# Broadcasts and scores over 128 rows, and a 31-tap convolution as column-group products, in a two-block network on one core

## The chip, the core and the metric

The kernel runs on 1 core of a Trainium2 chip. The metric is device time in microseconds (us), the median of the runs. TensorE is called PE in the profile, and PEld where it loads weights; VectorE is DVE, ScalarE is ACT, GpSimd is POOL, SyncE is SP.

## What is computed

The input `x` is 256 tokens of 1024 float32 numbers. The first block is a Mamba-2 layer (called SSD here), a convolutional feed-forward layer, an attention layer with forget gates (fox), and a second feed-forward layer. The second block puts 16 meta tokens ahead of the sequence (272 positions) and runs a mixer, then a layer of 16384 experts chosen by product keys. Cut to what the change touches:

```python
# SSD, per head: decay between positions of a chunk of 128
decay = exp(where(causal, a_cs[..., :, None] - a_cs[..., None, :], -inf))
# fox, per head
sc = q @ k.T * scale + cum[:, :, :, None] - cum[:, :, None, :]
# mixer of the second block: z = rmsnorm(h) @ w_in
h = a * sigmoid(b)                          # 512 channels, 272 positions
h = depthwise_conv(h, conv_w, taps=31, causal) + conv_b
conv_out = silu(layernorm(h))
attn_out = mla(z_q, z_kv, z_rope)           # 8 heads, low-rank queries and keys
h = h + concat(rmsnorm(attn_out), rmsnorm(conv_out)) @ w_out
# experts: 8 heads, two halves of 64 numbers, 128 keys each
s = einsum('chpd,hpnd->chpn', q, keys); top_k(s, 16) ...
```

## The kernel before

All large products split a float32 weight into a rounded part `hi` (ACT, L128) and a remainder `lo` (DVE, L129), both float32r, and the activations likewise; three float32r products stand for one float32 product. `mm_a` (L136 to L141) has the weights as the stationary operand and 256 or 272 tokens moving; `mm_b` (L143 to L147) has 128 tokens stationary and up to 512 weight columns moving. The stages run one after the other: `ssd`, `ffn(0)`, `fox`, `ffn(1)`, `mix2`, `peer`. Within a stage, `weave` places side work (attention steps, convolution pieces, routing) between weight blocks, and a static scheduler then fixes the order of each engine's instructions; each engine works through its own list in that order. SP issues the weight loads, ACT the small loads.

Broadcasts. `row_parts` (L364) keeps a row per head in a tile of 64 or 48 partitions: the rounded part in the low rows, the remainder 32 rows up. `rowbc` (L372, L375) spreads one head's row over 128 partitions by a product with a 0/1 column `pick` of as many rows. In SSD, `decay` does it for two heads at a time, each followed by a 128-row product that adds the mask (L377): 16 such places for 32 heads. In fox, `bias_item` does it for two heads at a time without the mask, 8 times.

Mixer (`mix2`). `low_rank` multiplies all tokens by 416 columns (L146 and its neighbours); the third tile, which holds the meta tokens, needs only the last 160 of them. `ab(f)` makes one quarter (128 channels) of the convolution's input `U[f]`. The 31 taps of quarter f are split at `PE_TAPS = (4, 4, 6, 31)`: the first ones on PE, where ACT scales an identity by the tap's weights (L821) and PE multiplies the shifted `U[f]` by it in float32 (L822); the others on DVE, one `scalar_tensor_tensor` each (L829). Attention is done in 16 steps of (query tile, head): `scores` (L964), a masked maximum on DVE (L968), two exponentials on ACT (L972, L973), a turn on PE (`flip`, L981), a copy on ACT (L983), `values` (L989). It is woven with the last two `ab` quarters and the convolution of quarters 1 and 2; quarter 3's convolution follows it, then `conv_done` (layer norm) and the output projection `out_proj` with the attention's four row blocks first.

Experts (`peer`). `route` computes the key scores for one token tile: `scores(p, hq)` multiplies 64 rows (half p) for four heads (L1106), 128 keys each, four times per token tile.

```python
            run(low_rank() + B[0])
            weave([queries] + B[1] + [key_values], C[0])
            weave(S, B[2] + C[1] + B[3] + C[2])
            run(C[3])
```

Of the kernel before, what the change touches and what calls it, by code (L numbers as in the profile page):

```python
# [10 lines left out]
F32 = mybir.dt.float32  # L11
F32R = mybir.dt.float32r
# [20 lines left out]
PE_TAPS = (4, 4, 6, 31)  # L33
# [13 lines left out]
for _n, _c in (("ssd_cw", 24 * 4), ("ssd_cb", 24), ("ffn_cw", 2 * FF * 3), ("ffn_cb", 2 * FF), ("c2w", 4 * CONV_K),  # L47
               ("c2b", 4), ("fox_qg", 1), ("fox_kg", 1), ("dt_bias", 1), ("a_log", 1), ("b_f", 1)):
    _cols(_n, _c)
# [17 lines left out]
def tile_body(ctx, tc, A, out):  # L67
# [23 lines left out]
    pick = const.tile([64, 32], F32R, name="pick")  # L91
# [147 lines left out]
    def out_proj(src, nk, yT, keep, fin=residual):  # L239

        acc = [ps_mm.tile([P, 512], F32, name="mm") for _ in range(4)]
        held = []

        def mms(j, w, t, cs=(0, 1)):
            hi, lo = w
            for c in cs:
                mm_b(acc[2 * t + c], yT, j, (t * P, (t + 1) * P), hi[:, c, :], lo[:, c, :], j == 0,
                     j == nk - 1)

        def item(j):  # L250
            h = j - (nk - len(keep))
            w = weight(src[j], 2, keep=keep[h]() if h >= 0 else None)
# [111 lines left out]
    def row_parts(pool, rows, name):  # L364

        n = rows.shape[0]
        r = pool.tile([n, T], F32R, name=name)
        nc.scalar.activation(r, rows, AF.Copy)
        nc.vector.tensor_tensor(r[32:], rows[32:], r[32:].bitcast(F32), op=OP.subtract)
        return r  # L370

    def rowbc(ps, rows, r, more=None):  # L372

        n = rows.shape[0]
        nc.tensor.matmul(ps, lhsT=pick[:n, r:r + 1].to_broadcast([n, P]), rhs=rows, start=True, stop=more is None)  # L375
# [18 lines left out]
    def ssd():  # L394
        with ExitStack() as es:
# [36 lines left out]
            nc.vector.tensor_tensor(pick, ident[:64, :32], ident[:64, 32:64], op=OP.add)  # L432
# [349 lines left out]
    def mix2():  # L782
        with ExitStack() as es:
# [16 lines left out]
            U, CP = {}, {}  # L800

            def ab(f):
                pre = []

                def second():
# [4 lines left out]
                    U[f] = sb.tile([P, TM + CONV_K - 1], F32, name=f"cu{f}")  # L810
                    nc.vector.memset(U[f][:, :CONV_K - 1], 0.0)
                    nc.vector.tensor_tensor(U[f][:, CONV_K - 1:], pre[0], sg, op=OP.mult)
# [3 lines left out]
            def taps_pe(f, j0, j1):  # L816
                if j0 == 0:
                    CP[f] = ps_mm.tile([P, 512], F32, name="mm")[:, :T]
                dg = sb.tile([P, j1 - j0, P], F32, name="dg", bufs=2)
                for j in range(j0, j1):  # L820
                    nc.scalar.activation(dg[:, j - j0, :], ident, AF.Copy, scale=col("c2w", f * CONV_K + j))  # L821
# [581 lines left out]
```

## Time and profile before

| | |
|---|---|
| median of 3 runs | 1724.05 us (1723.29 to 1724.34) |
| the profiled execution: its time, its span | 1724.77 us, 1723.0 us |
| PE busy | 1684.2 us, 98% |
| PEld busy | 1493.3 us, 87% |
| DVE busy | 1259.5 us, 73% |
| ACT busy | 966.2 us, 56% |
| POOL busy | 35.2 us, 2% |
| granted TensorE clock, mean | 0.998 of full speed |
| chain that ended last | PE 91%, DVE 4%, ACT 1%, DMA 1% |

The span is the time from the first to the last instruction of the program on the core; the execution's own time adds what lies around it. A row of the timeline gives the start of an instruction and its duration; products overlap in the array, so the distance between two starts, not the duration, is what a product costs. A float32 product is recorded twice, with half of its time each; a float32r product once.

### The profile page before, as it was taken

What the parts mean: (1) busy time and instruction counts of PE and PEld (TensorE: products, weight loads), DVE (VectorE), ACT (ScalarE), POOL (GpSimd) and SP (SyncE); (2) the same over time, 40 slices, a digit from 0 to 9 for tenths busy, and PEclk for the clock granted to TensorE, in tenths of its full rate; (3) what the DMA queues carried; (4) which work ended last, traced back from release to release, by engine and by line L of the source; (5) the groups of instructions that cost most, each with busy time, mean ns of one, the idle gap of its engine ahead of it and who ended that gap; (6) DMA issues with size and microseconds to landing.
All of it is one profiled execution on the core that took longest, in us unless ns stands there. A gap on an engine that the chain in (4) does not pass through costs nothing.

```text
span 1723.0 us, 28885 instructions
## 1 busy us (share of the span) xinstructions
PE 1684.2 (98%) x11035; PEld 1493.3 (87%) x11035; DVE 1259.5 (73%) x2581; ACT 966.2 (56%) x1425; POOL 35.2 (2%) x45
## 2 busy tenths in 40 slices
PE   6999999999999999999999999999999999999998
PEld 6878779998778799988988999999999988888886
DVE  5767667765765667747985998999999866666665
ACT  5678656554555665546765454546666644444443
POOL 0000000000110000001000000000000000000000
PEclk9999999999999999999999999999999999999999
DMA  5534345566354356664324666675555677777774
GB/s 189 183 110 138 109 152 176 184 199 225 107 155 154 117 160 186 207 203 152 114 97 160 206 235 211 223 232 179 176 175 167 220 238 236 236 242 236 241 239 151
DMA packets 87579, 315.30 MB, mean 183 GB/s; under 512 B 9984, under 2 KB 10368, under 8 KB 87312
## 3 DMA queue, kind: packets, MB, share of 16 engines
q1 hardware_dynamic: 80352, 290.36, 52.3%
q10 hardware_dynamic: 7088, 23.09, 3.6%
q8 instruction: 86, 1.41, 0.3%
q14 instruction: 53, 0.43, 0.1%
HBM read 295.59 MB, written 17.83 MB: 182 GB/s over the span
## 4 chain that ended last, share of the span: by engine, by line
PE 91%; DVE 4%; ACT 1%; issue 1%; DMA 1%; POOL 1%; SPq 0%; DVEq 0%; POOLq 0%; ACTq 0%
PE mm L1261 21%; PE mm L139 13%; PE mm L141 13%; PE mm L140 13%; PE mm L146 7%; PE mm L145 7%; PE mm L147 7%; PE pst L1220 3%; PE pst L171 1%; DVE lo L129 1%; PE pst L546 1%; PE pst L724 1%; PE pst L375 1%; PE pst L377 1%; PE po L749 1%
## 5 line engine op out<-in xcount | busy, mean ns | idle before, releaser
L129 DVE TENSOR_TENSOR lo<-raw,hi 128x1024 fp32r<-128x1024 f32 (+1 forms) x492 | 599.5, 1220 | 299.2 <-PE mm L1261 83.2
L128 ACT ACTIVATE hi<-raw 128x1024 fp32r<-128x1024 f32 (+1 forms) x492 | 519.4, 1057 | 505.3 <-PE mm L140 223.6
L139 PE MATMUL mm<-xT,hi 128*128 128x256 f32 (+1 forms) x1968 | 561.6, 285 | 1.2 <-DVE cacc L320 1.2
L141 PE MATMUL mm<-xT,lo 128*128 128x256 f32 (+1 forms) x1968 | 556.6, 283 | 1.9 <-DVE lo L129 1.9
L140 PE MATMUL mm<-xT,hi 128*128 128x256 f32 (+1 forms) x1968 | 551.3, 280 | 0.0
L139 PEld LDWEIGHTS mm<-xT,hi 128*128 128x128 f32 x1968 | 371.5, 189 | 4.7 <-issue 2.3
L141 PEld LDWEIGHTS mm<-xT,lo 128*128 128x128 f32 x1968 | 370.1, 188 | 3.0 <-DVE lo L129 2.5
L140 PEld LDWEIGHTS mm<-xT,hi 128*128 128x128 f32 x1968 | 371.1, 189 | 0.5
L1261 PE MATMUL mm<-hi,xT 128*128 128x512 f32 x992 | 270.0, 393 | 0.0
L1261 PEld LDWEIGHTS mm<-hi,xT 128*128 128x128 f32 x992 | 186.3, 188 | 42.6
L1261 PE MATMUL mm<-lo,xT 128*128 128x512 f32 x496 | 154.7, 392 | 0.0
L1261 PEld LDWEIGHTS mm<-lo,xT 128*128 128x128 f32 x496 | 93.1, 188 | 21.5
L145 PE MATMUL mm<-hi,xT 128*128 128x512 f32 (+1 forms) x240 | 96.7, 409 | 3.9 <-ACT xT L133 3.8
L147 PE MATMUL mm<-hi,xT 128*128 128x512 f32 (+1 forms) x240 | 95.2, 398 | 2.2 <-DVE xT L134 2.2
L146 PE MATMUL mm<-lo,xT 128*128 128x512 f32 (+1 forms) x240 | 96.1, 401 | 0.7 <-DVE lo L129 0.6
L320 DVE SCALAR_TENSOR_TENSOR cacc<-mm,pcol,cacc 128x255 f32<-128x255 f32 (+1 forms) x144 | 68.4, 480 | 13.6 <-ACT cacc L317 11.2
L1221 ACT ACTIVATE G<-pst 128x512 f32<-128x512 f32 x64 | 68.2, 1105 | 0.0
L1211 DVE TENSOR_TENSOR oo<-oo,slot 128x1536 bf16<-128x1536 bf16 x64 | 61.2, 957 | 1.7
L145 PEld LDWEIGHTS mm<-hi,xT 128*128 128x128 f32 x240 | 45.8, 192 | 14.3 <-ACT xT L133 5.4
L147 PEld LDWEIGHTS mm<-hi,xT 128*128 128x128 f32 x240 | 45.6, 190 | 12.3 <-DVE xT L134 4.1
L146 PEld LDWEIGHTS mm<-lo,xT 128*128 128x128 f32 x240 | 45.9, 191 | 9.7 <-DVE lo L129 2.3
L145 PE MATMUL mm<-hi,aT 128*128 128x512 f32 x136 | 53.9, 396 | 0.0
(406 smaller groups left out, 2121.5 us busy)
## 6 DMA issues: line engine op xcount, KB each, us to landing
raw<-in_u SPq DMA_DIRECT2D x128, 512.0 KB, 3.9
raw<-in_v SPq DMA_DIRECT2D x128, 512.0 KB, 4.3
raw<-in_w_up SPq DMA_DIRECT2D x88, 512.0 KB, 3.6
raw<-in_w_dn SPq DMA_DIRECT2D x44, 512.0 KB, 4.3
raw<-in_w_fox SPq DMA_DIRECT2D x32, 512.0 KB, 4.2
spill<-h ACTq DMA_DIRECT2D x30, 512.0 KB, 5.5
h<-spill SPq DMA_DIRECT2D x30, 512.0 KB, 4.8
raw<-in_w_xbc SPq DMA_DIRECT2D x24, 512.0 KB, 3.7
```

The source lines that it names most:

```text
L128: last[1] = nc.scalar.activation(hi[:, :width], raw[:, :width], AF.Copy)
L129: last[0] = nc.vector.tensor_tensor(lo[:, :width], raw[:, :width], hi[:, :width].bitcast(F32), op=OP.subtract)
L139: nc.tensor.matmul(ps, lhsT=hi[:, k, :], rhs=xT[:, k, 0, :], start=(k == 0), stop=False)
L140: nc.tensor.matmul(ps, lhsT=hi[:, k, :], rhs=xT[:, k, 1, :], start=False, stop=False)
L141: nc.tensor.matmul(ps, lhsT=lo[:, k, :], rhs=xT[:, k, 0, :], start=False, stop=(k == nk - 1))
L145: nc.tensor.matmul(ps, lhsT=xT[:, k, 0, c0:c1], rhs=whi, start=first, stop=False)
L146: nc.tensor.matmul(ps, lhsT=xT[:, k, 0, c0:c1], rhs=wlo, start=False, stop=False)
L147: nc.tensor.matmul(ps, lhsT=xT[:, k, 1, c0:c1], rhs=whi, start=False, stop=last)
L320: nc.vector.scalar_tensor_tensor(acc[:, d:], ps[:, :T - d], cw[:, j:j + 1], acc[:, d:], op0=OP.mult, op1=OP.add)
L1211: nc.vector.tensor_tensor(oo[:, 2:], oo[:, 1:2].to_broadcast([P, 3, P, NB]), cur[:, 2:, None].to_broadcast([P, 3, P, NB]), op=OP.mult)
L1221: nc.scalar.activation(G[:, :, t0:t0 + NB].rearrange("p i t -> p t i"), pg, AF.Copy)
L1261: nc.tensor.matmul(acc[2 * t + c], lhsT=w[x][:, t * P:(t + 1) * P], rhs=y[:, c, :], start=(i == 0 and x == 0 and y is b[0]), stop=(i == P ...
```

## The change

- `pick` and the rows of `row_parts` get 128 partitions; POOL sets the unused rows to zero (L369 of the changed kernel), and `rowbc` multiplies over all 128 rows.
- `keys` holds, for each head and half, the 64 rows of the half and zeros in the other 64; `scores(hq)` makes both halves of two heads by one 128-row float32 product of 256 columns each.
- The convolution: `U[f]` (now `u`, two buffers) goes to DRAM and comes back as `V[f]`, in which the 128 partitions hold 4 shifts of 32 channels, for 4 groups q of 32 channels. `DG[f]` (POOL, L831) holds, for 8 groups m of 4 taps and each q, the 128x32 matrix of the taps' weights. `taps(f)` (L841) adds 8 products into each of the 4 groups of 32 output partitions: 32 products of 128 rows, 32 columns and 256 positions. All loads and stores of this are issued by POOL.
- The order of `mix2`: all `ab` quarters and the convolution of quarter 0 come ahead of attention; the convolution of quarters 1 to 3, `conv_done` and the first two blocks of the output projection are woven into it; the projection takes the convolution's four row blocks first.
- `low_rank` computes only columns 256 to 416 of the meta tile.

```diff
     def row_parts(pool, rows, name):
-        r = pool.tile([n, T], F32R, name=name)
-        nc.scalar.activation(r, rows, AF.Copy)
+        r = pool.tile([P, T], F32R, name=name)
+        nc.gpsimd.memset(r.bitcast(F32), 0.0)
+        nc.scalar.activation(r[:n], rows, AF.Copy)
...
     def rowbc(ps, rows, r, more=None):
-        nc.tensor.matmul(ps, lhsT=pick[:n, r:r + 1].to_broadcast([n, P]), rhs=rows, start=True, stop=more is None)
+        nc.tensor.matmul(ps, lhsT=pick[:, r:r + 1].to_broadcast([P, P]), rhs=rows, start=True, stop=more is None)
...
+            eye = sb.tile([P, 32], F32, name="eye")
+            nc.vector.tensor_tensor(eye, ident[:, :32], ident[:, 32:64], op=OP.add)
+            for q in (64, 96):
+                nc.vector.tensor_tensor(eye, eye, ident[:, q:q + 32], op=OP.add)
...
+                    d = dram.tile([P, UW], F32, name=f"cud{f}")
+                    nc.gpsimd.dma_start(d, u)
+                    V[f] = sb.tile([P, 4, UW - 3 - NM], F32, name="cv", bufs=2)
+                    for s in range(4):
+                        nc.gpsimd.dma_start(V[f][32 * s:32 * s + 32],
+                                            d[:, NM + s:UW - 3 + s].rearrange("(q c) t -> c q t", q=4))
+                    if f % 2 == 0:
+                        DG["tile"] = sb.tile([P, 2, 4 * NTAP, 32], F32, name=f"dg{f // 2}")
+                    DG[f] = DG["tile"][:, f % 2]
+                    with tc.issue_after(i.ins):
+                        nc.gpsimd.tensor_tensor(DG[f], eye[:, None].to_broadcast([P, 4 * NTAP, 32]),
+                                                col("c2w", 4 * NTAP * f, 4 * NTAP)[:, :, None]
+                                                .to_broadcast([P, 4 * NTAP, 32]), op=OP.mult)
...
+            def taps(f):
+                pc = ps_t.tile([P, 512], F32, name="pst")[:, :T]
+                for m in range(NTAP):
+                    for q in range(4):
+                        nc.tensor.matmul(pc[32 * q:32 * q + 32], lhsT=DG[f][:, q * NTAP + m],
+                                         rhs=V[f][:, q, 4 * m:4 * m + T], start=(m == 0),
+                                         stop=(m == NTAP - 1))
+                nc.scalar.activation(cT[:, f, :], pc, AF.Identity, bias=col("c2b", f))
...
-                            mm_b(acc[i][:, :416], xT, k, tiles[i], hi[:, j, :], lo[:, j, :], k == 0, k == KD - 1)
+                            n0 = 256 if i == 2 else 0
+                            mm_b(acc[i][:, n0:416], xT, k, tiles[i], hi[:, j, n0:], lo[:, j, n0:], k == 0, k == KD - 1)
...
-            weave([queries] + B[1] + [key_values], C[0])
-            weave(S, B[2] + C[1] + B[3] + C[2])
+            run([queries] + B[1] + [key_values] + B[2] + C[0] + B[3])
+            o = out_proj(A["w_out2"], KD, mT, keep_tiles(sb, 3, "qT2", "dg0", "dg1"), order=[4, 5, 6, 7, 0, 1, 2, 3])
+            weave(S, C[1] + C[2] + C[3] + [lambda: conv_done(0), lambda: conv_done(1)] + o[:2])
...
-                            nc.tensor.matmul(ps[:, j, :], lhsT=qT[p * HM:(p + 1) * HM, hq + j, t * P:(t + 1) * P],
-                                             rhs=keys[p * HM:(p + 1) * HM, hq + j, :], start=True, stop=True)
+                                             lhsT=qT[:, hq + j, t * P:(t + 1) * P],
+                                             rhs=keys[:, hq + j].rearrange("p a n -> p (a n)"), start=True, stop=True)
```

In the stages `ssd`, `ffn` and `fox` the order of every engine's list stays as it was, apart from the zeroing on POOL. In `mix2` it moves. POOL's list, before, from the norm of the meta tokens (L154) to the attention's norms (L859); L232 is the reciprocal root for one token tile's norm, `stat`:

```order
L154 TENSOR_TENSOR rstd<-ms,nhalf 16x1
L232 TENSOR_TENSOR stat<-stat,nhalf 128x2 x2
L859 TENSOR_TENSOR nr<-nss,nhalf 128x1 x7
L154 TENSOR_TENSOR rstd<-ms,nhalf 128x1 x2
L859 TENSOR_TENSOR nr<-nss,nhalf 128x1 x2
```

And of the change, from the same place:

```order
L154 TENSOR_TENSOR rstd<-ms,nhalf 16x1
L232 TENSOR_TENSOR stat<-stat,nhalf 128x2
L817 MEMSET cu 128x30
L818 MEMSET cu 128x1
L817 MEMSET cu 128x30
L818 MEMSET cu 128x1
L831 TENSOR_TENSOR dg_7986<-eye,pcol 128x1024
L232 TENSOR_TENSOR stat<-stat,nhalf 128x2
L831 TENSOR_TENSOR dg_7986<-eye,pcol 128x1024
L831 TENSOR_TENSOR dg_8311<-eye,pcol 128x1024 x2
L868 TENSOR_TENSOR nr<-nss,nhalf 128x1 x5
L822 DMA cud_7979<-cu 128x303
```

The first `DG` stands between the two tiles' `stat`. DVE's list of the change at the same place, where L230 makes the input of the second `stat` and L805 the last step of `eye`, which `DG` reads:

```order
L194 TENSOR_SCALAR stat<-stat 128x1
L134 TENSOR_TENSOR xT<-pst,xT 128x4x128
L231 COPY stat<-stat 128x1
L805 TENSOR_TENSOR eye<-eye,ident 128x32
L194 TENSOR_SCALAR stat<-stat 128x1
L805 TENSOR_TENSOR eye<-eye,ident 128x32
L968 MEMSET za_7723 128x112
L230 SCALAR_TENSOR_TENSOR stat<-stat 128x1
```

Before, the same rows stand there without the two of `eye`. PE's list, before, in the first third of attention (L139 to L141 are an `ab` block, L822 a convolution piece):

```order
L139 MATMUL mm<-xT,hi 128x272
L140 MATMUL mm<-xT,hi 128x272
L141 MATMUL mm<-xT,lo 128x272
L989 MATMUL po<-v_7715,pT 128x64 x2
L964 MATMUL pst<-kT_7714,qT_7713 128x144
L981 MATMUL pst<-ident,za_7719 128x128 x2
L822 MATMUL mm<-cu_8146,dg 128x256 x4
L989 MATMUL po<-v_7715,pT 128x64 x2
```

And of the change, from the last `ab` product to the first piece of quarter 1's convolution (L975, L992, L1000 are now `scores`, `flip`, `values`):

```order
L141 MATMUL mm<-xT,lo 128x272
L975 MATMUL pst<-kT_7720,qT_7719 128x144 x2
L992 MATMUL pst<-ident,za_7723 128x128
L975 MATMUL pst<-kT_7720,qT_7719 128x144
L992 MATMUL pst<-ident,za_7723 128x128
L992 MATMUL pst<-ident,za_7724 128x128
L975 MATMUL pst<-kT_7720,qT_7719 128x144
L992 MATMUL pst<-ident,za_7724 128x128
L1000 MATMUL po<-v_7721,pT 128x64 x2
L992 MATMUL pst<-ident,za_7725 128x128
L841 MATMUL pst<-cv,dg_7986 32x256
L992 MATMUL pst<-ident,za_7725 128x128
```

Attention's first steps now follow one another with nothing between them; the four convolutions stand in six pieces in all (32; 1 and 31; 1 and 31; 32), each between products of the whole array.

## Rows read from the trace of the kernel before

**Rows 1.** The page, busy time, share of the span, instructions.
```profile
PE 1684.2 (98%) x11035; PEld 1493.3 (87%) x11035; DVE 1259.5 (73%) x2581; ACT 966.2 (56%) x1425; POOL 35.2 (2%) x45
```
**Rows 2.** Windows: SSD's woven part, then the mixer; columns as in their heads.
```profile
core 0: us, PE busy (x) PEld busy (x) DVE busy (x) ACT busy (x) POOL busy (x), PEclk, DMA share, GB/s
80.00:213.00 133.00, 128.15 (x711) 102.36 (x710) 90.96 (x136) 97.95 (x165) 3.86 (x3) 0.99 0.38 126
789.00:916.00 127.00, 123.24 (x752) 108.10 (x751) 105.00 (x272) 86.31 (x234) 9.13 (x14) 1.00 0.35 117
```
**Rows 3.** Timeline of PE in SSD: start, duration, line, operation, out<-in, shapes.
```profile
81.58 0.38 PE L375 MATMUL pst<-acsr,pick 64*128 64x256 f32 x1
81.89 0.39 PE L377 MATMUL pst<-later,identr 128*128 128x256 f32 x1
...
82.73 0.28 PE L139 MATMUL mm<-xT,hi 128*128 128x256 f32 x1
82.85 0.28 PE L140 MATMUL mm<-xT,hi 128*128 128x256 f32 x1
```
**Rows 4.** Timeline of PE in fox, two of the eight bias items.
```profile
457.35 0.73 PE L375 MATMUL pst<-cumr,pick 48*128 48x256 f32 x4
458.01 0.50 PE L145 MATMUL mm<-hi,xT 128*128 128x512 f32 x1
458.34 0.40 PE L146 MATMUL mm<-lo,xT 128*128 128x512 f32 x1
458.58 0.39 PE L147 MATMUL mm<-hi,xT 128*128 128x512 f32 x1
```
**Rows 5.** Timeline of PE at the first of eight key-score groups.
```profile
940.99 0.28 PE L141 MATMUL mm<-xT,lo 128*128 128x256 f32 x1
941.20 1.16 PE L1106 MATMUL pst<-keys,qT 64*128 64x128 f32 x8
942.28 0.39 PE L139 MATMUL mm<-xT,hi 128*128 128x256 f32 x1
942.50 0.28 PE L140 MATMUL mm<-xT,hi 128*128 128x256 f32 x1
```
**Rows 6.** Timeline of PE in fox: scores of heads in both halves of the rows.
```profile
482.57 0.72 PE L724 MATMUL pst<-qkT,qkT 64*128 64x128 f32 x8
483.22 0.50 PE L146 MATMUL mm<-lo,xT 128*128 128x512 f32 x1
```
**Rows 7.** Timeline of PE in the mixer: four taps, then an `ab` block.
```profile
818.90 1.89 PE L822 MATMUL mm<-cu,dg 128*128 128x256 f32 x8
820.43 0.47 PE L139 MATMUL mm<-xT,hi 128*128 128x272 f32 x1
820.75 0.29 PE L140 MATMUL mm<-xT,hi 128*128 128x272 f32 x1
```
**Rows 8.** Groups of the whole span, by form: busy, mean ns of one.
```profile
L829 DVE SCALAR_TENSOR_TENSOR cT<-cu,pcol,cT 128x256 f32<-128x256 f32 x79 | 37.4, 481 | 0.7
L822 PE MATMUL mm<-cu,dg 128*128 128x256 f32 x90 | 21.8, 382 | 0.0
```
**Rows 9.** Timeline of PE in the mixer's `low_rank`.
```profile
800.10 0.35 PE L147 MATMUL mm<-hi,xT 128*128 128x416 f32 x1
800.28 0.35 PE L145 MATMUL mm<-hi,xT 128*128 128x416 f32 x1
```
**Rows 10.** Timelines of POOL, DVE and PE: the second tile's norm.
```profile
793.34 0.70 POOL L232 TENSOR_TENSOR stat<-stat,nhalf 128x2 f32<-128x2 f32 x1 [5.40 <-DVE stat L230]
794.08 0.75 DVE L209 SCALAR_TENSOR_TENSOR hn<-h,stat,gain 128x512 f32<-128x512 f32 x1 [0.65 <-POOL stat L232]
794.98 0.30 PE L171 MATMUL pst<-ident,hn 128*128 128x128 f32 x1 [0.22 <-DVE hn L209]
```
**Rows 11.** Groups of the whole span: POOL and DVE elementwise.
```profile
L84 POOL IOTA jmp<- 128x128 f32 x1 | 0.2, 238 | 0.4 <-POOLq L1395 0.4
L129 DVE TENSOR_TENSOR lo<-raw,hi 128x1024 fp32r<-128x1024 f32 x486 | 593.6, 1223 | 298.1 <-PE mm L1261 83.2 <-PE mm L146 78.3 <-PE mm L141 76.4
```

More of the change, by code (lines that the diff above doesn't have):

```diff
@@ L32 @@
 CONV_K = 31
-PE_TAPS = (4, 4, 6, 31)
+NTAP = 8
 CD = 0
@@ L237, in keep_tiles, with out_proj @@
                 for name in [*names, *(f"keep{j}" for j in range(n - len(names)))]]
-    def out_proj(src, nk, yT, keep, fin=residual):
+    def out_proj(src, nk, yT, keep, fin=residual, order=None):
+        order = order or list(range(nk))
         acc = [ps_mm.tile([P, 512], F32, name="mm") for _ in range(4)]
@@ L251, in item @@
             h = j - (nk - len(keep))
-            w = weight(src[j], 2, keep=keep[h]() if h >= 0 else None)
+            w = weight(src[order[j]], 2, keep=keep[h]() if h >= 0 else None)
             mms(j, w, 0)
@@ L827, in taps_v @@
[L827 to L835 removed]
+                    u = sb.tile([P, UW], F32, name="cu", bufs=2)
@@ L1036, in conv_done @@
                 defer(rest, CD)
-            C = [conv_items(f) for f in range(4)]
+            C = [[lambda f=f: taps(f)] for f in range(4)]
             B = [ab(f) for f in range(4)]
@@ L1083, in peer @@
                 s1 = e1.enter_context(tc.tile_pool(name="peer_r", bufs=1))
-                keys = s1.tile([P, 8, P], F32, name="keys")
-                nc.scalar.dma_start(keys, A["keys"])
+                keys = s1.tile([P, 8, 2, P], F32, name="keys")
+                for p in range(2):
+                    nc.gpsimd.memset(keys[(1 - p) * HM:(2 - p) * HM, :, p], 0.0)
+                    nc.scalar.dma_start(keys[p * HM:(p + 1) * HM, :, p], A["keys"][p * HM:(p + 1) * HM])
                 qT = s1.tile([P, 8, T], F32, name="qT")
@@ L1170, in route @@
                     out = []
-                    for p in range(2):
-                        for hq in range(0, 8, 4):
-                            out.append((0.1, lambda p=p, hq=hq: scores(p, hq)))
-                            for j in range(4):
-                                out.append(lambda p=p, hq=hq, j=j: best(SC[p, hq][:, j, :], P, sv[:, p, hq + j],
+                    for hq in range(0, 8, 2):
+                        out.append((0.1, lambda hq=hq: scores(hq)))
+                        for j in range(2):
+                            for p in range(2):
+                                out.append(lambda p=p, hq=hq, j=j: best(SC[hq][:, j, p, :], P, sv[:, p, hq + j],
                                                                         si[:, p, hq + j]))
@@ L1366, in _layout @@
     put("ffn_cb", g["ffn_conv_b"].reshape(2, FF, P).transpose(2, 0, 1))
-    put("c2w", g["conv_w_2"][0].reshape(CONV_K, 4, P).transpose(2, 1, 0))
+    w = np.concatenate([g["conv_w_2"][0].reshape(CONV_K, 512), np.zeros((1, 512), np.float32)])
+    put("c2w", w.reshape(NTAP, 4, 16, 32).transpose(1, 3, 2, 0).reshape(P, -1))
     put("c2b", g["conv_b_2"][0].reshape(4, P).T)
```

61 lines of the change are left out of this document (20 added, 41 removed).

## The prediction

> **What bounds the kernel now.** The page first: PE is busy 98% of the span, DVE 73%, ACT 56%, POOL 2% [rows 1]. Then the table of windows: in SSD's woven part and in the mixer PE is also the busiest engine, with 4.9 us idle of 133 and 3.8 of 127 [rows 2]. A term counts, then, if it shortens PE's own list; work taken from DVE or ACT counts only where PE waited for it. But "busy" covers time in which the array drains, and this shows in the timeline of PE, by the distance of starts. Two plain products of 256 columns start 0.12 us apart (82.73 and 82.85). Where a product of 64 rows and one of 128 alternate, they start 0.31 apart [rows 3]. So each passage between the two row heights costs 0.19 us. Four key-score products of 64 rows also pay on the way in and out: 0.21 from the last whole-array product to the first, and 0.22 after the way out, where 0.12 is usual [rows 5].
>
> **The change part by part.** All rows are of the profiled execution (1724.77 us), so the sum is made against that; the median is 0.72 lower.
>
> *SSD broadcasts.* From the first broadcast to the second product after the place is 1.27 us (81.58 to 82.85) for five distances; at 0.12 each they would take 0.60. The way in adds 0.09 (0.21 less 0.12, as in rows 5). That is 0.76 a place, 16 places: 12.2 us of PE. Nothing else is removed: moving columns stay 256, and the zeroing on POOL is one small operation long before. Not all need come through, since DVE and ACT are busy 91 and 98 us of these 133 [rows 2], and the 4.9 us of PE's idle time there show that they end last in places; if those waits grow by as much again, 7.3 is left. I take 10.5, nearer the upper end because the two engines still have over 20 us to spare.
>
> *Fox broadcasts.* Two items take 0.99 us (457.35 to 458.34) for four products and the next one [rows 4]; four at 0.12 and one 512-column product at 0.24 (458.34 to 458.58) are 0.72. With the way in that saves 0.36; the 8 items stand in 6 places of the timeline: 2.2. I take 2.0.
>
> *Key scores.* A group takes 1.51 us from 940.99 to 942.50 [rows 5]. Changed, it is two float32 products of 256 columns without a passage. Such a product costs two records of 0.216: eight records and the next start lie from 818.90 to 820.75, less one 0.12 step, 1.73 for eight [rows 7]. So 0.12 + 4 x 0.216 + 0.12 = 1.10, and 8 groups save 3.3. The weight blocks on both sides follow without a wait, so I take all of it.
>
> *Convolution.* Removed: 90 records on PE [rows 8], 19.4 us at 0.216, and 79 DVE operations of 481 ns, which lie beside PE and count as nothing unless PE waits. Added: 128 products, 256 records. What they cost hangs on whether the four column groups run at once. No row shows column groups. The nearest rows are products of two row halves: eight records that alternate between the halves take 0.65 us to the next product (482.57 to 483.22) [rows 6], where eight records of the same size that keep to one half take 1.08 (941.20 to 942.28) [rows 5]. Halves do run together. By that, four at once: 64 sets of 0.216, 13.8 us, plus six visits to another array shape at 2 x 0.19, 2.3: 16.1, a gain of 3.3. The other bound is one at a time: 256 x 0.216 + 2.3 = 57.6, a loss of 38.2. I take the first, by the nearest row.
>
> The Trainium skill says against it ("TensorE: Matmul & The Clock Gate", Part 3, The mechanism) that a weight load overlaps running products only when its row group differs, and these four share all rows. By that rule it would be one at a time, and the sum 41.5 us higher. This trace does not bear it out for the whole array: product and load time add up to 3177 us in a span of 1723 [rows 1], with the same rows throughout.
>
> *Meta tile.* 24 products of 416 columns start 0.18 to 0.19 apart [rows 9]. With 160 columns they can't go below 0.12, a step for 256 columns; 24 x 0.07 = 1.7. But 9 of them stand ahead of the second tile's turn, for which PE waits already (0.22, rows 10), so 0.6 turns into wait: 1.1 is left. Narrow float32r products are not in the trace; at the float32 rate they would take 2 x 0.216 x 160/256 = 0.27, a loss of 1.9. I take the gain.
>
> *POOL's list.* The first DG stands ahead of the second `stat`, and its input `eye` is ready only 0.2 to 0.3 us before that `stat` (the order of DVE). So the whole of it, less 0.2, delays `stat` (793.34), DVE's `hn` (794.08) and PE's turn (794.98), which has no cover left [rows 10]. Its cost: DVE does as many elements in 1.2 us; POOL's index row of 128 elements takes 0.238, so 1024 take 1.9 [rows 11]. I take 1.9, it being POOL's own row: 1.7 lost. Twice as much would be 3.6. The other three run while `low_rank` goes on.
>
> The Trainium skill ("GPSIMD Engine Reference", § 3.1 Elementwise) puts POOL at 2.6 cycles an element at 1.2 GHz for two inputs, by which I estimate 2.2 us, and the sum would be 0.3 higher; no run here shows it yet.
>
> *Attention.* Before, `ab` blocks lay between its steps; now its first steps stand alone. From a score to its turn the work passes DVE and ACT, and from the turn to `values` ACT again. A like passage over two engines takes 1.6 us (793.34 to 794.98) [rows 10]; two of them, 3.2, less some 10 small products at 0.12 or less: 2.0 lost, between 0 and 3.2. Later steps have 32 convolution products in each gap. The last quarter's reload waits for `taps(1)` to free its buffer; behind that PE has `taps(2)`, 16 sets of 0.216 or 3.5 us, and some 25 small products, 2 to 3. I put nothing on it, up to 2 in the range. The same for the tail: the projection starts inside attention, and its cover for the last norm is 18 products of 0.24.
>
> Sum: -10.5 - 2.0 - 3.3 - 3.3 - 1.1 + 1.7 + 2.0 = -16.5. From 1724.77 that gives 1708.3, and 0.7 lower for the runs: **1707.5 us**.
>
> **The rivals.**
> (1) *Column groups one at a time.* Place: the four `taps`. For it: no row shows such groups at once. Against: row halves do run at once [rows 6]. Price: 41.5 us above my sum, 1749, slower. It decides below 1.8 at a time: the rest of the sum gives 13.2 us, and 55.3/n + 2.3 may then reach 32.6.
> (2) *Two at a time,* as the only case that the trace has: 27.6 + 2.3 = 29.9, 13.8 above my sum: 1721.3, within what can be told from no change.
> (3) *POOL becomes the late one.* It now builds DG, and issues 20 transfers, each waiting in its list for the one ahead; if DG takes twice my value and each of quarters 1 to 3 is 2 to 3 us late, some 9 us are lost: 1717. Against: ahead of quarter 0 stand two `ab` quarters, 96 products at 0.12 or 11.5 us, besides the queries and keys.
> (4) *The 0.31 us are not the passage but the broadcast column* (a stride of zero), and stay: 12.5 us of gain go, 1720. Against: the key scores pay the same on the way in and out, with plain operands [rows 5].
>
> **How the numbers follow.** My case 0.61, (1) 0.14, (2) 0.10, (3) 0.10, (4) 0.05. About 0.2%, 3.4 us, can be told from no change. The low end: 12.2 for SSD, 1.7 for the meta tile, no passages at the convolution, no loss at attention's start: about 8 lower, 1699. The high end takes in the lower bounds of SSD (+3.2), meta (+3.0), DG (+1.9), attention (+1.2) and the reload (+2), and cases (3), (4) and (2): 1721. Left out are (1) and some 5% of the rest. Faster: my case, (3) and half of (4), 0.74; same, mostly (2), 0.10; slower 0.16.
>
> **What would show it.** Right: starts of L376 and its mask products 0.12 apart in SSD, and SSD shorter by about 10 us; four L841 records within a few hundredths of a us, then 0.2 to the next four; PE idle about 2 us ahead of the second tile's turn; the mixer about as long as before. Wrong: L841 records 0.2 apart one by one (the mixer then 40 us longer), or SSD's gain taken back as waits for DVE and ACT.

## The result, and the profile after

The changed kernel takes 1732.88 us (median of 9 runs, 1729.58 to 1737.85) against 1724.05 for the kernel before (9 runs, 1721.18 to 1726.54): a ratio of 1.0060, interval 1.0045 to 1.0074 (the ratios here are taken over all runs; that of the two medians alone is 1.0051). It is slower, and lies above the range of the prediction. Its profiled execution took 1730.78 us, 2.1 below the median, and has a span of 1728.7 us, against 1723.0. The page's busy line, to be read against [rows 1]:

```profile
PE 1671.9 (97%) x11169; PEld 1482.8 (86%) x11169; DVE 1233.8 (71%) x2501; ACT 952.0 (55%) x1380; POOL 58.4 (3%) x81
```

PE is busy 12 us less, and the span is 5.7 us longer: the work shrank and the waiting grew. To find where, the program is cut at products that both profiles have. The first product of all starts at another time in each profile (9.53 us before, 7.70 after), so stretches are compared and not clock times. The three columns on the right are runs that the next section tells of.

| stretch on PE, us | before | changed | rows alone | products late, old end | projection behind transposes |
|---|---|---|---|---|---|
| first product to the last of SSD's output | 233.7 | 223.2 | 224.8 | 226.9 | 223.3 |
| to the last of fox's projection (the first FFN and fox) | 353.2 | 352.0 | 352.8 | 352.5 | 352.3 |
| to the last of the second FFN | 192.2 | 192.6 | 193.1 | 194.3 | 192.9 |
| `low_rank`, to the first product on `cqT` | 25.8 | 32.7 | 25.5 | 25.4 | 25.3 |
| to the first attention score | 22.4 | 35.8 | 22.3 | 37.5 | 20.5 |
| to the first transpose in `conv_done` | 49.4 | 28.6 | 49.4 | 47.7 | 48.4 |
| to the last product of the projection | 24.6 | 46.4 | 24.8 | 26.0 | 26.1 |
| the mixer, sum of these four | 122.1 | 143.5 | 121.9 | 136.5 | 120.2 |
| to the first key score | 30.4 | 30.7 | 30.1 | 30.2 | 30.2 |
| first to last key score | 135.1 | 132.0 | 132.0 | 132.0 | 132.0 |

What was made for 128 rows gained: 10.5 us in SSD, 1.3 in the row that ends with fox (fox by itself 1.0, from 161.7 to 160.8), 3.1 at the key scores. The mixer lost 21.4. SSD's row also varies by execution, with the clock: before and in the changed kernel 3.4 us of it lie at 1.2 GHz, in the rows alone 6.8, in the column beside it 10.2. In the six profiled executions of changed kernels with 3.4 us, SSD takes 222.5 to 223.3 us, a gain of 10.4 to 11.2. First the gains, in the timeline of PE after (start, duration, line, operation, out<-in, shapes), as [rows 3, 5]:

```profile
78.75 0.36 PE L376 MATMUL pst<-acsr,pick 128*128 128x256 f32 x1
78.95 0.28 PE L378 MATMUL pst<-later,identr 128*128 128x256 f32 x1
79.07 0.28 PE L376 MATMUL pst<-acsr,pick 128*128 128x256 f32 x1
79.18 0.28 PE L378 MATMUL pst<-later,identr 128*128 128x256 f32 x1
79.30 0.28 PE L139 MATMUL mm<-xT,hi 128*128 128x256 f32 x1
...
949.50 0.29 PE L141 MATMUL mm<-xT,lo 128*128 128x256 f32 x1
949.63 1.03 PE L1116 MATMUL pst<-keys,qT 128*128 128x256 f32 x4
950.30 0.47 PE L139 MATMUL mm<-xT,hi 128*128 128x256 f32 x1
950.61 0.28 PE L140 MATMUL mm<-xT,hi 128*128 128x256 f32 x1
```

The starts in SSD are 0.11 to 0.12 us apart behind the first distance (0.20), where they were 0.31 [rows 3]; a key-score group takes 1.11 us (949.50 to 950.61) where it took 1.51 [rows 5]. The convolution, in the same view, where 0.216 us a record was the price before [rows 7]:

```profile
834.22 3.66 PE L841 MATMUL pst<-cv,dg 128*32 128x256 f32 x64
837.81 0.39 PE L139 MATMUL mm<-xT,hi 128*128 128x272 f32 x1
...
851.46 5.13 PE L841 MATMUL pst<-cv,dg 128*32 128x256 f32 x62
856.52 0.66 PE L1000 MATMUL po<-v,pT 128*128 128x64 f32 x4
...
859.75 3.65 PE L841 MATMUL pst<-cv,dg 128*32 128x256 f32 x62
863.33 0.51 PE L975 MATMUL pst<-kT,qT 96*128 96x144 f32 x2
```

64 records in 3.59 us are 16 sets of four, 0.224 us a set: the four column groups run at once, and one record costs 0.056. Within a set the four starts are some 0.006 us apart, and the next set follows 0.195 behind. The second visit shown is slower (5.06 us for 62, against 3.58 in the third); the clock is lower there, as shown below. The Trainium skill's rule ("TensorE: Matmul & The Clock Gate", Part 3, The mechanism), that a weight load overlaps running products only where its row group differs, is not borne out: these four share all rows, and their 64 loads of 0.11 us each, 7.0 us in all, went with those 3.59 us.

So the products came out as costed. Where the mixer lost is in the windows (to be read against [rows 2]) and in the waits of PE (us in total, times, longest). There, `hn` is a token tile's normed input, `on` a normed output of the attention or the convolution, `za` the softmax's exponentials and `pT` the same after their turn:

```profile
core 0: us, PE busy (x) PEld busy (x) DVE busy (x) ACT busy (x) POOL busy (x), PEclk, DMA share, GB/s
775.70:808.20 32.50, 25.24 (x145) 22.68 (x145) 23.53 (x59) 12.77 (x31) 13.12 (x14) 0.84 0.34 108
808.20:846.00 37.80, 36.21 (x296) 31.71 (x294) 18.59 (x37) 22.21 (x42) 8.77 (x19) 1.00 0.70 191
846.00:872.50 26.50, 24.90 (x261) 15.93 (x262) 4.93 (x30) 12.11 (x50) 2.74 (x5) 0.87 0.21 67
872.50:900.00 27.50, 18.86 (x114) 15.98 (x111) 15.16 (x41) 14.29 (x43) 2.75 (x5) 0.88 0.02 3
```
```profile
PE pst L171 <- DVE on L871: 7.9, 3, 5.1
PE pst L171 <- DVE hn L209: 5.3, 2, 4.4
PE pst L992 <- ACT za L983: 2.5, 1, 2.5
PE po L1000 <- ACT pT L994: 1.4, 2, 0.9
```

The longest wait of PE in the mixer before:

```profile
PE mm L147 <- DVE xT L134: 1.0, 1, 1.0
```

So no wait was over 1.0 us then, and the clock stood at 1.00 [rows 2]. Now three places wait, and during or right behind each of these waits the granted clock falls to 1.2 GHz. Windows laid on those three stretches:

```profile
782.90:793.00 10.10, 6.80 (x23) 5.74 (x24) 9.03 (x6) 2.00 (x3) 6.29 (x3) 0.50 0.21 65
847.70:854.40 6.70, 6.70 (x41) 3.65 (x44) 1.02 (x7) 2.80 (x14) 0.00 (x0) 0.50 0.25 91
878.50:885.10 6.60, 4.12 (x15) 3.57 (x16) 2.65 (x7) 2.48 (x6) 0.55 (x1) 0.50 0.01 2
```

PE works 17.6 us at half speed in them, so some 9 us (half of that, an estimate) come on top of 17.1 us of named waits. The three places:

**The second norm.** POOL, DVE and PE in the changed kernel, then DVE at the same place before, as [rows 10]:

```profile
780.12 1.91 POOL L831 TENSOR_TENSOR dg<-eye,pcol 128x1024 f32<-128x1024 f32 x1 [3.81 <-DVE eye L805]
781.98 0.70 POOL L232 TENSOR_TENSOR stat<-stat,nhalf 128x2 f32<-128x2 f32 x1
782.65 6.54 POOL L831 TENSOR_TENSOR dg<-eye,pcol 128x1024 f32<-128x1024 f32 x3
...
782.72 4.71 DVE L209 SCALAR_TENSOR_TENSOR hn<-h,stat,gain 128x512 f32<-128x512 f32 x2 [2.30 <-POOL stat L232]
787.46 2.29 DVE L790 TENSOR_SCALAR h<-h,stat 128x1024 f32<-128x1024 f32 x1
...
785.25 1.09 PE L171 MATMUL pst<-ident,hn 128*128 128x128 f32 x4 [4.37 <-DVE hn L209]
```
```profile
794.08 1.42 DVE L209 SCALAR_TENSOR_TENSOR hn<-h,stat,gain 128x512 f32<-128x512 f32 x2 [0.65 <-POOL stat L232]
795.53 0.76 DVE L789 TENSOR_SCALAR h<-h,stat 128x1024 f32<-128x1024 f32 x1
```

The first DG takes 1.91 us, as predicted, and holds `stat` up. But then DVE's two `hn` take 4.71 us where they took 1.42, and the next operation 2.29 where it took 0.76: each lasts as long as the DG that POOL runs beside it.

**The attention's start** (843.94 on): PE waits 2.5 us for the softmax, since the two value-and-gate blocks (the last two `ab` quarters) that lay between its steps before are done ahead of it.

**The convolution's norm**, now in PE's list between two steps of the attention, in the timeline of PE:

```profile
875.01 0.88 PE L1000 MATMUL po<-v,pT 128*128 128x64 f32 x6 [0.93 <-ACT pT L994]
880.98 1.33 PE L171 MATMUL pst<-ident,on 128*128 128x128 f32 x5 [5.09 <-DVE on L871]
```

The turns of `on` stand ahead of the next scores, and the chain behind `conv_done` (means and variances on DVE, tanh and square on ACT, powers on POOL, DVE between and behind them) takes from 872.58 to 880.98.

### The profile page after: what moved, and what is told of

It reads as the page before. It is cut to its first block, busy times and chain, and to the rows that moved or that the text cites. A ratio compares the mean times of both kernels' runs of the same rounds, so it can differ in the third digit from the quotient of the medians.

```text
span 1728.7 us, 29105 instructions
## 1 busy us (share of the span) xinstructions
PE 1671.9 (97%) x11169; PEld 1482.8 (86%) x11169; DVE 1233.8 (71%) x2501; ACT 952.0 (55%) x1380; POOL 58.4 (3%) x81
## 4 chain that ended last, share of the span: by engine, by line
PE 88%; DVE 5%; ACT 3%; issue 1%; DMA 1%; POOL 1%; SPq 0%; DVEq 0%; POOLq 0%; ACTq 0%
PE mm L1272 20%; PE mm L139 13%; PE mm L141 13%; PE mm L140 13%; PE mm L145 6%; PE mm L146 6%; PE mm L147 6%; PE pst L1231 3%; PE pst L841 1%; PE pst L171 1%; DVE lo L129 1%; PE pst L725 1%; ACT hi L128 1%; PE pst L547 1%; DMA raw<-in_w_pq 1%
## 5 line engine op out<-in xcount | busy, mean ns | idle before, releaser
L139 PE MATMUL mm<-xT,hi 128*128 128x256 f32 (+1 forms) x1968 | 561.8, 286 | 1.2 <-DVE cacc L321 1.2
L141 PE MATMUL mm<-xT,lo 128*128 128x256 f32 (+1 forms) x1968 | 557.0, 283 | 1.9 <-DVE lo L129 1.9
L139 PEld LDWEIGHTS mm<-xT,hi 128*128 128x128 f32 x1968 | 371.7, 189 | 4.4 <-issue 2.7
L141 PEld LDWEIGHTS mm<-xT,lo 128*128 128x128 f32 x1968 | 370.2, 188 | 2.9 <-DVE lo L129 2.5
L1272 PEld LDWEIGHTS mm<-lo,xT 128*128 128x128 f32 x496 | 93.2, 188 | 21.4
L145 PE MATMUL mm<-hi,xT 128*128 128x512 f32 (+2 forms) x240 | 95.8, 405 | 4.5 <-ACT xT L133 3.9
L146 PE MATMUL mm<-lo,xT 128*128 128x512 f32 (+2 forms) x240 | 96.0, 400 | 2.2 <-DVE lo L129 2.2
L147 PE MATMUL mm<-hi,xT 128*128 128x512 f32 (+2 forms) x240 | 95.1, 398 | 1.8 <-DVE xT L134 1.7
L147 PEld LDWEIGHTS mm<-hi,xT 128*128 128x128 f32 x240 | 46.0, 192 | 12.2 <-DVE xT L134 4.1
```

What stands on the lines that cost most here:

```text
L139: nc.tensor.matmul(ps, lhsT=hi[:, k, :], rhs=xT[:, k, 0, :], start=(k == 0), stop=False)
L141: nc.tensor.matmul(ps, lhsT=lo[:, k, :], rhs=xT[:, k, 0, :], start=False, stop=(k == nk - 1))
L145: nc.tensor.matmul(ps, lhsT=xT[:, k, 0, c0:c1], rhs=whi, start=first, stop=False)
L146: nc.tensor.matmul(ps, lhsT=xT[:, k, 0, c0:c1], rhs=wlo, start=False, stop=False)
L147: nc.tensor.matmul(ps, lhsT=xT[:, k, 1, c0:c1], rhs=whi, start=False, stop=last)
L1272: nc.tensor.matmul(acc[2 * t + c], lhsT=w[x][:, t * P:(t + 1) * P], rhs=y[:, c, :], start=(i == 0 and x == 0 and y is b[0]), stop=(i == P ...
```

## The experiments

Medians are of the runs of each kernel; all ratios are against the kernel before, run on the same chip (its medians 1723.94 to 1724.33). No edit leaves out part of the computation. The changed kernel's interval is 2.5 us to either side, so a gain counted from its median is good to some 3 us. The mixer of each profiled execution is a second measure, free of what SSD and the other stages do:

| kernel or run | mixer, us |
|---|---|
| before; changed; rows alone (run 3) | 122.1; 143.5; 121.9 |
| runs 1; 2; 4 (products late; old end; both) | 140.0; 140.1; 136.5 |
| runs 7; 12 (cover back; and weights on VectorE) | 134.3; 128.3 |
| runs 5; 8; 9; 10 | 129.5; 129.0; 125.9; 124.5 |
| runs 13; 14 | 120.2; 122.0 |
| runs 6; 11 (the rows alone with POOL products; with the wide third product) | 129.1; 122.7 |

**1. The POOL products behind their quarter's store.**

```
-                    nc.gpsimd.dma_start(d, u)
+                    g = nc.gpsimd.dma_start(d, u)
-                    with tc.issue_after(i.ins):
+                    with tc.issue_after(g.ins):
```

> Each POOL product that builds a set of column-group weights (1.91 us in the changed kernel's trace) is issued after the store of its own quarter, and so behind the second norm's power on POOL and no longer ahead of it; nothing else moves. Theory (three separate losses: POOL's list at the low-rank blocks, the clock falling after the wait, the norm chain in the middle of the attention): the stretch from the mixer's first product to the first transposed query goes from 32.5 us back to 24 to 26 us, the granted clock stays at 2.4 GHz in it, and the whole is 6 to 9 us below the changed kernel, near 1725. Rival (the 22 us that the mixer grew by belong to the convolution's new form, its products and its loads, and the order costs little): less than 3 us below the changed kernel, 1730 or more.

1729.94, ratio 1.0031 (1.0021 to 1.0041): 2.9 us less by the medians and 3.5 by the mixer, at the rival's edge and not the 6 to 9 of the theory. The stretch itself did what the first theory says: 25.3 us, clock 1.00. But 3.9 us came back later, where the products now run. DVE and POOL of this run, then PE's waits that are new:

```profile
807.50 4.45 DVE L129 TENSOR_TENSOR lo<-raw,hi 128x1024 fp32r<-128x1024 f32 x2 [0.78 <-PE mm L146]
...
807.79 1.93 POOL L831 TENSOR_TENSOR dg<-eye,pcol 128x1024 f32<-128x1024 f32 x1
...
PE mm L141 <- DVE lo L129: 1.6, 1, 1.6
...
PE pst L975 <- DVE mx L979: 1.3, 1, 1.3
```

Two splits of weights take 4.45 us, 2.0 more than two at 1.22 [rows 11], beside a product of 1.93. Moving a POOL product moves the place where DVE stands still; it does not remove it.

**2. The old end of the mixer.**

```
-            o = out_proj(A["w_out2"], KD, mT, keep_tiles(sb, 3, "qT2", "dg0", "dg1"), order=[4, 5, 6, 7, 0, 1, 2, 3])
-            weave(S, C[1] + C[2] + C[3] + [lambda: conv_done(0), lambda: conv_done(1)] + o[:2])
+            weave(S, C[1] + C[2] + C[3])
             load_gain("ffn2_g")
-            run(o[2:4])
             flush()
+            o = out_proj(A["w_out2"], KD, mT, keep_tiles(sb, 3, "qT2", "dg0", "dg1"))
+            conv_done(0)
+            conv_done(1)
+            run(o[:4])
+            flush()
```

> The end of the mixer alone goes back to the order before: the convolution's norms are begun with the output projection, whose first four blocks in their own order cover them, and the attention is woven with three quarters of the convolution only. Theory: the waits of 5.3 and 2.8 us on the norm chain between the attention's products go, and with them most of the 6.8 us at 1.2 GHz that follow, which cost half their length; 8 to 11 us below the changed kernel, near 1723. Rival (the norms are late wherever they stand, since the chain itself takes 8 us and the first four blocks now cover less): below the changed kernel by less than 3 us, with a wait of 3 us or more on the norm in the projection instead.

1728.55, ratio 1.0026 (1.0016 to 1.0035): 4.3 us less. The waits on `on` fell from 7.9 to 2.0 us, as the theory says, but half of the gain expected did not come. The wait for the softmax (2.5 us) stayed, and some 10 us of the attention behind it, no longer 7, ran at 1.2 GHz (the clock is 0.88 over 44.3 us). The two projection blocks that the new end puts between the attention's steps had gone; that this is why is not shown.

**3. The rows alone:** the 128-row broadcasts and scores and the narrow third product, with the old convolution, its order and the old end.

> The 128-row broadcasts, the 128-row key scores and the narrower third product of the low-rank blocks, with the convolution, its order and the output projection of before. Theory: all that the change gains stands here; the state-space block 12, the second block 1.3, the scores 3.1 and the third product 1 to 2 us, together 17 to 19, so 1705 to 1707. Rival (the gains of the parts that start earlier are partly lost at the next wait on a load): 1711 or more.

1711.21, ratio 0.9928 (0.9911 to 0.9945). All the gain stands here, but it is 13 us and not 17 to 19: in SSD 8.9 us in this execution, with 6.8 us of it at 1.2 GHz, where I had read 12 off clock times that began 1.8 us apart. No wait on a load took it, so the rival's number came without its reason.

**4. Edits 1 and 2 together.**

> The two edits together: the POOL products behind their stores, and the end in the order before. Theory: two separate losses, so the gains add: 14 to 20 us below the changed kernel, 1713 to 1719; what then remains above the rows alone is the start of the attention (a wait of 2.7 us and 6.8 us at 1.2 GHz) and the convolution's own passages. Rival (one cause behind both): not more than the larger of the two alone.

1726.94, ratio 1.0016 (1.0003 to 1.0028): 5.9 us less, and far from what was expected. The two add up: in the mixer 3.5 and 3.4 us apart, 7.0 together. Its mixer is still 14.4 us longer than before. The attention, from the first score to `conv_done`, before and in this run:

```profile
836.80:886.20 49.40, 49.17 (x335) 45.19 (x334) 43.54 (x126) 39.65 (x131) 1.27 (x2) 1.00 0.23 76
```
```profile
845.50:893.00 47.50, 42.20 (x358) 30.71 (x357) 16.62 (x61) 25.51 (x92) 5.81 (x8) 0.82 0.18 52
```

Two value-and-gate blocks of some 6 us each were moved out of this stretch, and by the table it is only 1.7 us shorter. PE idles 5.3 us, and the clock is at 1.2 GHz for a good third. This led to the next theory: the blocks were cover, that is, work of PE beside the attention's chains on DVE and ACT.

**5. Edit 4, and the blocks back in the attention.**

```
-            run([queries] + B[1] + [key_values] + B[2] + C[0] + B[3])
+            run([queries] + B[1] + [key_values])
-            weave(S, C[1] + C[2] + C[3])
+            weave(S, B[2] + C[0] + B[3] + C[1])
             load_gain("ffn2_g")
+            run(C[2] + C[3])
```

> The products behind their stores and the old end as in the run with both edits, and besides the last two of the four value-and-gate blocks (12 us of products) go back into the attention, each followed by a quarter of the convolution, the other two quarters behind the attention. Theory, formed from the run with both edits, whose attention lost 16 to 17 us to waits on its softmax and to 17 us at 1.2 GHz: those blocks were the attention's cover, and with them back TensorE hardly waits and the clock stays up. The 14 us by which that run's mixer is longer than before go, and some 3 us of convolution come as a gain: 1708 to 1713. Rival (the four-group products themselves pull the clock down and wait on their loads, wherever they stand): 1720 or more.

1718.48, ratio 0.9971 (0.9959 to 0.9982): 8.5 us less than run 4, and faster than before. The direction speaks for cover, and the waits for the softmax are gone. The size was some half of what the theory said (1708 to 1713), so neither range held: 7 us above the rows alone remain, with PE waiting 4.7 us on `on`, 1.6 on a split of weights and 1.1 on the last quarter's load.

**6. The rows alone with four idle POOL products.**

```
+                    extra = sb.tile([P, 32, 32], F32, name="ex")
+                    with tc.issue_after(i.ins):
+                        nc.gpsimd.tensor_tensor(extra, ident[:, None, :32].to_broadcast([P, 32, 32]),
+                                                ..., op=OP.mult)
```

(The norm's tile `ln` is laid into another to make room.)

> The rows alone (1711.2), with four POOL products of 128x1024 added that nobody reads; the order puts all four between the first and the second norm's power on POOL. The output is unchanged by them. Theory (POOL's list holds the second norm up, and VectorE's work on two operands stands still beside each product): the stretch from the mixer's first product to the first transposed query grows from 25.5 us by 6 to 12 us, and the clock falls in it; 1717 to 1723. Rival (the products lie beside other work, and the loss seen came from the convolution's other parts): 1711 to 1713.

1716.95, ratio 0.9961 (0.9950 to 0.9973): 5.7 us more than the rows alone, with nothing of the new convolution in it. The stretch grew from 25.5 to 32.9 us, clock 0.84. POOL and DVE:

```profile
778.97 8.54 POOL L816 TENSOR_TENSOR ex<-ident,pcol 128x1024 f32<-128x1024 f32 x4 [1.40 <-issue]
...
779.12 2.32 DVE L790 TENSOR_SCALAR h<-h,stat 128x1024 f32<-128x1024 f32 x1
781.35 0.68 DVE L225 TENSOR_TENSOR hn<-mm,h 128x512 f32<-128x512 f32 x1
...
782.08 1.67 DVE L226 TENSOR_TENSOR h<-hn,gain 128x512 f32<-128x512 f32 x1
783.67 0.68 DVE L134 TENSOR_TENSOR xT<-pst,xT 128x512 fp32r<-128x512 f32 x1
```

Operations of 512 columns or more that read only SBUF are held (L790 takes 2.32 us for 0.76, L226 1.67 for 0.68); those with one operand in PSUM (`mm`, `pst`) keep their 0.68 us. All four products stand ahead of the second `stat` here and only one in the changed kernel, so the loss is not made up in the same way in both: PE waits 3.7 us for an operation of DVE and 2.0 for `hn`.

**7. The changed kernel with only the blocks put back** (`weave(S, B[2] + C[0] + B[3] + C[1] + ...`, its end new, its products early).

> The changed kernel with only the two value-and-gate blocks put back into the attention, its POOL products early and its end new, with the convolution's norms in the middle of the attention's list. Theory: the attention's start gets its cover back (waits of 2.7 and 1.1 us, 6.8 us at 1.2 GHz), but the norm chain's wait stays: 5 to 12 us below the changed kernel, 1721 to 1728. Rival (cover is not the point, the norm chain and POOL are all of it): within 2 us of the changed kernel.

1723.62, ratio 1.0001 (0.9991 to 1.0010): 9.3 us less than the changed kernel (9.2 in the mixer), the largest single undoing. PE's waits, then the window of the attention, from the first score to `conv_done`:

```profile
PE pst L171 <- DVE hn L209: 5.3, 2, 4.4
PE pst L171 <- DVE on L871: 4.8, 2, 4.3
...
830.00:870.70 40.70, 40.41 (x458) 32.99 (x457) 14.19 (x51) 23.48 (x78) 7.06 (x15) 1.00 0.44 129
```

The wait for the softmax is gone, and PE idles 0.3 us in the window at full clock. That on `hn` stays; those on `on` fall from 7.9 to 4.8 us, so some 3 of the 9 us belong to the convolution's norm and not to the attention's start.

**8. Run 5 with the weights built on VectorE** (`nc.vector.tensor_tensor(DG[f], ...` after the gated product).

> As the run with products late, old end and cover back, but the column-group weights are built on VectorE, 1.22 us each by the nearest row, and POOL is left free. Theory (VectorE is held for the whole of a POOL product of 1.9 us): 1 to 3 us below the run it starts from, since four holds of 1.9 us become four of 1.2 and no other work stands still. Rival (VectorE's own list now carries 5 us more in front of the splits of the weights): equal or up to 2 us above it.

1716.49, ratio 0.9951 (0.9934 to 0.9967): 2.0 us less than run 5 by the medians, the size of the first theory, but the intervals overlap and the mixers differ by 0.5 us: not told apart. PE still waits 4.8 us on `on` and 0.7 on the last quarter's load.

**9. Run 8 with the quarters issued earlier** (`weave(S, C[0] + B[2] + C[1] + B[3] + C[2])`, then `C[3]`).

> The run with cover back and weights on VectorE, with the convolution's quarters issued earlier in the attention: the first quarter ahead of the third value-and-gate block, the second ahead of the fourth, the third behind it, and only the last behind the attention. Theory: what is left above the rows alone (1716.5 against 1711.2) is that the last quarter's load waits for a buffer that the second quarter still reads, so the last product comes 3 us later than the old convolution's, and everything behind it is a chain (norm, transposes, four blocks of the projection, next norm); with the buffer free earlier 2 to 5 us less, 1711 to 1714. Rival (the chain behind the last product is as long as ever, and the lighter convolution leaves TensorE nothing to do beside it): 1715 or more.

1715.34, ratio 0.9947 (0.9934 to 0.9961), not told apart from run 8: by its number the rival. The wait on the load and one on `on` are gone, one of 2.7 us on `on` stays.

**10. Run 8 with three load buffers** (`name="cv", bufs=3`, with `cu` and `sg` at one, `cq` in `on`).

> The run with cover back and weights on VectorE, with three buffers instead of two for the shifted rows (one instead of two for the two tiles that lead to them, and the query norm's tile laid into another, to make room); the order as there. Theory (the load of the last quarter is late): the wait of about 1 us on that load goes, the last product comes 2 to 4 us earlier; 1712 to 1715. Rival (the load is not what decides): 1716 to 1717.

1712.72, ratio 0.9933 (0.9920 to 0.9947): 3.8 us less than run 8 (4.5 in the mixer), as the theory says, though its interval overlaps that of run 8. The wait on the load is gone; what stays is 2.7 us on `on`, in the projection.

**11. The rows alone without the narrow third product.**

> The rows alone with the third product of the low-rank blocks over all 416 columns again, as before. Theory: the narrower product saved nothing, since the stretch ends on the second norm's wait either way (25.5 us in the rows alone, 25.6 to 25.8 before): 1711 to 1712. Rival (24 products that are 0.09 us shorter count in full): 2 us above the rows alone, 1713 or more.

1710.29, ratio 0.9923 (0.9910 to 0.9937): by the medians no gain from the narrow product. The traces leave room for a small one: the `low_rank` stretch takes 26.3 us here, 25.8 before and 25.5 in the rows alone, where PE waits 0.92 us for the second norm and not 0.22.

**12. Run 7 with the weights on VectorE.**

> The changed kernel with its new end, the two blocks back in the attention, and the weights built on VectorE, so that POOL's list holds no product. Theory: what is left against the rows alone is the norm chain in the attention's list (a wait of 4.5 us and the clock at 1.2 GHz behind it, some 8 us together) less a few us for the lighter convolution: 5 to 7 us below the run with cover back alone, 1716 to 1719. Rival (POOL's early products cost nothing once the cover is back): 1722 or more.

1716.10, ratio 0.9948 (0.9935 to 0.9962): 7.5 us less than run 7 (6.0 in the mixer), and the wait on `hn` falls from 5.3 to 1.4 us. With cover in place, that is what the weights cost more on POOL than on VectorE. The longest wait on `on`, in the attention, stays at 4.3 us (the profiled execution, 1722.27 us, is the slowest of its five). This kernel with the new end and run 8 with the old one can't be told apart (1716.10 and 1716.49), so the 4.3 us of run 2 hold for the changed kernel and not once cover and POOL are put right.

**13. Run 10 with the projection held behind the transposes,** and **14. the quarters earlier too.**

```
-            conv_done(1)
-            run(o[:4])
+            with tc.issue_after(conv_done(1).ins):
+                run(o[:4])
```

> The run with three load buffers, with the output projection's first four blocks held behind the transposes of the convolution's sums. Theory (what is left is cover, and it was spent too early): the wait of 2.9 us and the 6.8 us at 1.2 GHz behind it go, 2 to 5 us less, 1708 to 1711, at or below the rows alone. Rival (the chain behind the last product decides, and the products would only stand idle elsewhere): 1712 or more, with a wait ahead of the convolution's last quarter or of the transposes in place of the one removed.

1709.70, ratio 0.9925 (0.9911 to 0.9939). The last waits on `on` are gone from the list, and the windows of its four stretches show the clock at 1.00 all through:

```profile
777.70:803.00 25.30, 22.02 (x145) 20.41 (x144) 19.13 (x61) 12.78 (x31) 4.65 (x8) 1.00 0.44 136
803.00:823.50 20.50, 20.36 (x138) 17.97 (x137) 14.35 (x29) 15.47 (x34) 5.56 (x12) 1.00 0.65 192
823.50:872.00 48.50, 47.37 (x509) 38.94 (x508) 21.67 (x69) 30.81 (x99) 7.22 (x17) 1.00 0.41 122
872.00:898.00 26.00, 24.82 (x113) 18.94 (x111) 18.52 (x31) 12.73 (x22) 3.70 (x5) 1.00 0.46 151
```

> The same with the convolution's quarters issued earlier in the attention, so that only the last stands behind it. Theory: the last product then comes up to 3 us earlier, 1706 to 1710. Rival (the last attention norm then lacks cover): equal to the run before it or up to 2 us above.

1710.12, ratio 0.9924 (0.9911 to 0.9938): equal, the rival. So the column-group convolution costs nothing in itself, and gains almost nothing: the mixer of run 13 is 1.7 us shorter than that of the rows alone, that of run 14 as long (122.0 and 121.9), and the medians of runs 3, 11, 13 and 14 can't be told apart. All four beat the kernel before by 13 to 14 us and the changed kernel by over 20.

## Why the prediction was wrong

The four terms of the mixer (convolution, meta tile, POOL's list, attention's start) came to a gain of 0.7 us in the sum; the mixer lost 21.4. That is 22 of the 25 us between 1707.5 and 1732.9, and the other terms were near.

*SSD, fox, key scores* (10.5, 2.0, 3.3): 10.5, 1.0 and 3.1 in the changed kernel, for the reason given. That SSD came out at 10.5 is in part luck: it was a choice between 7.3 and 12.2, and executions with the same clock gave 10.4 to 11.2, the rows alone 8.9. In fox two of the six places gained nothing.

*Convolution* (3.3, four groups at once): right in mechanism. 0.224 a set, against 0.216 taken. Rivals (1) and (2) fall by the 64 records in 3.59 us, rival (4) by the starts 0.12 us apart. But the term was read as if PE's list alone counted: with every cover restored 1.7 us of it came in run 13 and nothing in run 14.

*Meta tile* (1.1): the medians of runs 3 and 11 show none of it, their traces 0.8 us and that against the kernel before 0.3. The narrow products are quick (three take 0.30 us, where three at 0.19 took 0.57; "can't go below 0.12" was wrong), but the wait for the second norm grew by 0.7, as the term had allowed.

*POOL's list* (1.7 lost): the step that said a DG costs only its own length ahead of `stat`. The length was right (1.91, in part by luck, since an index row of 128 elements was another kind of operation; the estimate of 2.2 from the Trainium skill, "GPSIMD Engine Reference", § 3.1 Elementwise, is too high for these operands), and the rest was missing. "The other three run while `low_rank` goes on" put nothing on what they do to DVE, and no term had the clock in it. Run 6 puts the loss at 5.7 us without the convolution, run 12 at 7.5 with it, against weights on VectorE. A page of the Trainium skill that I had not weighed says it ("SBUF — State Buffer", Who interferes with whom): a VectorE instruction with two SBUF inputs contends with a GpSimd instruction that reads SBUF, since its second input comes through an interface that the two share and that only one holds at a time. Run 1 agrees (4.45 us for 2.44 beside a product of 1.93), and so do `hn` (4.71 for 1.42) in the changed kernel and L226 in run 6. L790, which has one tensor as input, is held too; that sentence does not cover it.

*Attention's start* (2.0 lost, 0 to 3.2): the largest error. The step costed the first wait only, 2.5 us in the trace, and took "later steps" as covered by the convolution. Putting the two blocks back is worth 9.3 us alone and 8.5 beside the other edits: the wait, what follows at 1.2 GHz, the later steps, each a chain over DVE and ACT with little PE work beside it, and in run 7 some 3 us of the wait on the convolution's norm. How the rest divides between them no run shows.

*The tail* (nothing): "its cover for the last norm" looked at the last norm, while the late one was the convolution's, which the change had moved into the attention's list with nothing behind it that PE could go on with. Run 2 puts that at 4.3 us with what else the old end brings, in the changed kernel alone: with the cover back and POOL free, runs 8 and 12 don't tell the two ends apart.

The profile before did show the common cause: PE was busy 123 of 127 us in the mixer [rows 2], so cover and work were nearly equal there. Removing work and moving 12 us of it forward left the chains of DVE, ACT and POOL bare. Rival (3), POOL as the late one, had one of the right engines but the wrong way: it named late transfers, and PE waits for none of them in the changed kernel, for 0.7 us in run 8 and 1.1 in runs 5 and 13. The low end of the range was added up wrongly: its four terms (1.7, 0.6, 2.3, 2.0) make 6.6 and not about 8. Nothing hangs on it.

## To carry to other kernels

Where PE is busy all through a stretch and DVE and ACT form chains beside it, count the work of PE as cover: before blocks are moved forward, go along each chain that they lay beside and ask which products are left for its time. A long operation put on POOL was paid for on DVE as well, wherever a long operation of DVE beside it read only SBUF. A wait of a few us on PE is to be priced with the slower products that follow it.

## What the runs showed of the hardware

- Four float32 products on the four column groups, all over the same 128 rows, run at once: 256 columns of four in 0.224 us, where one over the whole array takes 0.216. 62 records that began at 1.2 GHz took 5.06 us instead of 3.58.
- DVE operations of 512 columns or more that read only SBUF last as long as the POOL product beside them (0.7 became some 2.4 us, 0.76 became 2.3), and the POOL product beside them took up to 2.36 us instead of 1.91; DVE operations with an operand in PSUM did not change (0.68).
- During or right behind waits of 4.4, 2.5 and 5.1 us on PE the granted clock fell to 1.2 GHz for 10, 7 and 7 us; in the mixer of run 13, where no wait of PE was over 1.3 us, it stayed at 2.4 GHz. No limit follows from this: in the changed kernel's SSD, 3.4 us at 1.2 GHz came behind two waits of 1.7 and 1.0 us that lie 2 us apart.
